# Scan stage of a hybrid SSD and ConvFFN layer: in-chunk products in pinned runs of four chunks, decay shift and clamp on ScalarE, state chain first in a step

## The chip, the cores and the metric

The kernel runs on one NeuronCore of a Trainium2 chip, as one launch. The metric is the device time of one execution in microseconds (us). A core has a matrix engine (TensorE, in the profile PE, with its weight loads as PEld), a vector engine (VectorE, DVE), a scalar engine (ScalarE, ACT), a general engine (GpSimd, POOL) and a queue processor that issues DMA transfers (SyncE, SP). Each takes its own instructions in order; semaphores tie them together. TensorE reads from the on-chip memory SBUF and writes to the banks of PSUM; the other compute engines move results out of PSUM.

## The reference

One layer of a flow-matching backbone with 1024 channels, for 1024 latent tokens and 128 context tokens. The part that matters here is the state space scan (SSD) of the first sub-layer. For each of 32 heads of 64 channels, each direction, and each chunk of 128 tokens:

```
a_cs = cumsum(dt * A) inside the chunk
L = exp(where(i >= j, a_cs[i] - a_cs[j], -inf))
CB = C @ B^T                                   (one per group of 8 heads)
y_diag = (CB * L) @ (x * dt)                   products inside the chunk
states = B^T @ (exp(a_cs[-1] - a_cs) * x * dt) what the chunk adds to the state
h[k+1] = exp(a_cs[-1]) * h[k] + states         the chain over chunks
y_off = (C * exp(a_cs)) @ h[k]                 what earlier chunks give
y = y_diag + y_off, both directions, + D * x
```

There are eight latent chunks, which start from a given state, and one context chunk, which starts from zero and whose final states are outputs. Before the scan stand a norm, a modulation and one input projection (`h @ w_in`), with a convolution and a SiLU on x, B and C. After it come a gate with SiLU(z), a gated norm, a second branch (a spatial gating MLP), the merge, and the ConvFFN.

## The kernel before, in words

**Number format.** Large products are made of three matmuls of split numbers (`gemm_cm`, L295 to L303: high times high, high times low, low times high). The products of the scan are plain float32 matmuls; the trace shows each of them as two records.

**Projection units.** One unit (`inproj`, L425) makes one tile of 128 output channels for all 1152 tokens, in three blocks of 384 tokens with 24 matmuls each (`gps`, 72 in all). There are three PSUM banks for them (`pg`). A unit's sink takes the block out of PSUM, and between blocks other work is emitted.

**The scan.** The 32 heads are handled as 16 pairs `q`. Pair q has tiles X (its x, channel-major, three buffers), Xtok (the same by tokens), and shares B, C and CB with its group of four pairs. The nine chunks are handled in five stages `s`: stages 0 to 3 have two latent chunks each, stage 4 is the context chunk. Parts of the work are:

- `ssd_loads` (L632): a DMA on SP's queue brings the cumulative sums into every partition (R, three buffers; E, two buffers), and the starting state into H.
- `mstage` (L662), the decays of one stage: R plus a bias per row (`nb`, which holds log dt minus the cumulative sum), limited to 60, through exp, times CB, both directions added into the first half of R. Of eight shifts of 128x128, the first NACT = 4 run on ScalarE and need a clamp of their own on VectorE (L677); the others do shift and clamp in one VectorE instruction (L674).
- `chain` (L697), in four steps: weighted x (`xwf`, `xwb`), its product with B into PSUM (`pst`, a single bank), then H[k+1] = decay * H[k] + product on VectorE.
- `ctx_state` (L717): the same for the context chunk (`pstc`, in the same single bank), out to the outputs.
- `main` (L729): the products with the state (`yo`, one bank), the products inside the chunks (`yd`, one bank; 64 columns wide, because each head has 64 channels, the two heads of a pair in the two column halves), then VectorE puts E * yo, D * x and yd together in X.

**Order of the work.** `pro` and `outs` (L765 to L767) list the steps of a pair; `merge` (L770) spreads the steps of outs(q) and pro(q+1) over the projection units of round q. The framework then orders each engine's instructions by priority, that is by place in the program, as soon as what they need is there in its own plan. `tc.high_priority(offset=P_SCAN)` moves the steps ahead of their place by 50; decays at the start have 200. `queue_behind` (L274) places one instruction behind another on its engine, without a semaphore. `z_unit(q-1)`, one round later, multiplies the finished X by SiLU(z) and stores it.

Of the kernel before, what the change touches and what calls it, by code (L numbers as in the profile page):

```python
# [14 lines left out]
NL = 1024  # L15
# [17 lines left out]

NGATE = [1, 1, 1, 0, 1, 1, 1, 0, 1, 1, 1, 0, 1, 1, 1, 0, 0]

NACT = 4

NXM, NWM, GBUF = 4, 10, 7

LAG0 = 12  # L40

LASTK = 4

P_SCAN, P_HT, P_MOD, P_DECAY = 50, 100, 200, 200


def gcol(t):
# [61 lines left out]
def body(tc, A, O):  # L109
# [338 lines left out]
    k_cm, kp = pool("tok")  # L448
    nb = kp.tile([128, NC, 64], F32, name="nb")
    wst = kp.tile([128, NC, 64], F32, name="wst")  # L450
    cdk = kp.tile([128, 8, 2, 32], F32, name="cdk")
    sb_cm, spb = pool("ssdB")
    u_cm, up = pool("dt")
# [29 lines left out]
    def decays():  # L483
        for src, dst in ((xd, dtt), (xa, adt)):
            ps = tbank("pdt")
            for i in range(4):
                PE.transpose(ps[:, 128 * i:128 * i + 128], src[:, 128 * i:128 * i + 128], ident)
            pv = ps.rearrange("p (c m) -> p c m", m=128)
            S.copy(dst[:, 0:4, :], pv[:, :, 0:64])
            V.tensor_copy(dst[:, 5:9, :], pv[:, :, 64:128])  # L490
        ps = tbank("pdt4")
        for j, src in enumerate((xd, xa)):
            PE.transpose(ps[:, 128 * j:128 * j + 128], src[:, 512:640], ident)
        for j, dst in enumerate((dtt, adt)):
            V.tensor_copy(dst[:, 4, :], ps[:, 128 * j:128 * j + 64])
        for d in range(2):
            a_d = adt[:, :, 32 * d:32 * d + 32]
            for lhs, dst in (((Lo, Up)[d], acst), (ones, tot)):
                pv = tbank(f"pacs{d}")[:, :288].rearrange("p (c h) -> p c h", h=32)
                PE.matmul(pv, lhsT=lhs, rhs=a_d, start=True, stop=True)  # L500
                V.tensor_copy(dst[:, :, 32 * d:32 * d + 32], pv)
        rows = up.tile([64, NC, 128], F32, name="rows")
        for b in range(3):
            ps = tbank(f"prow{b}")
            for i in range(3):
                PE.transpose(ps[:64, 128 * i:128 * i + 128], acst[:, 3 * b + i, :], ident)
            V.tensor_copy(rows[:, 3 * b:3 * b + 3, :], ps[:64, :384].rearrange("p (c m) -> p c m", m=128))
        for d in range(2):
            for h in range(2):
                SP.dma_start(acs_scr[:, d, h], rows[32 * d + h:32 * d + 32:2, :, :])  # L510
        V.tensor_scalar(lndt, dtt, 1e-18, None, op0=ALU.max)
        S.activation(lndt, lndt, AF.Ln)
        V.tensor_tensor(nb, lndt, acst, op=ALU.subtract)
# [115 lines left out]

    Rt, EPt, Ht = {}, {}, {}  # L630

    def ssd_loads(q, s):  # L632

        cc = cc_of(s)
        n = len(cc)
        R = spa.p.tile([128, 2, 2, 2, 128], F32, tag="R", name=f"R{q}{s}", bufs=3)
        if n == 2:
            SP.dma_start(R.rearrange("p d h c i -> p (d h) (c i)"),
                         acs_scr[q, :, :, cc[0]:cc[0] + 2].rearrange("d h c i -> (d h) (c i)").unsqueeze(0).to_broadcast([128, 4, 256]))
# [4 lines left out]
        if s < 4:  # L644
            E = spa.p.tile([128, 2, 2, 128], F32, tag="EP", name=f"EP{q}{s}", bufs=2)
            for h in range(2):
                SP.dma_start(E[64 * h:64 * h + 64].rearrange("p d c i -> p d (c i)"),
                             acs_scr[q, :, h, cc[0]:cc[0] + 2].rearrange("d c i -> d (c i)").unsqueeze(0).to_broadcast([64, 2, 256]))
            EPt[q, s] = E
        if s == 4:  # L650
            H = spa.p.tile([128, 8, 2, 128], F32, tag="H", name=f"H{q}", bufs=2)
            SP.dma_start(H[:, 0], A["h0"][q])
            Ht[q] = H

    def ssd(q):

# [1 line left out]
        _, Bt, CT, CB = groups[g]  # L658
        X, Xt = xq[q]
        Dc = par[:, P_D + q:P_D + q + 1]  # L660

        def mstage(s):  # L662
            cc = cc_of(s)
            n = len(cc)
            R = Rt[q, s]
            for d in range(2):
                for h in range(2):
                    col = 32 * d + 2 * q + h
                    for i, c in enumerate(cc):
                        r = R[:, d, h, i, :]  # L670
                        if 4 * d + 2 * h + i < NACT:
                            S.activation(r, r, AF.Identity, bias=nb[:, c, col:col + 1])  # L672
                        else:
                            V.tensor_scalar(r, r, nb[:, c, col:col + 1], 60.0, op0=ALU.add, op1=ALU.min)  # L674
            Rv = R.rearrange("p d h c i -> p (d h) c i")[:, :, :n]
            if NACT:
                V.tensor_scalar(Rv[:, :NACT // 2], Rv[:, :NACT // 2], 60.0, None, op0=ALU.min)  # L677
            S.activation(Rv, Rv, AF.Exp)
            if s < 4:
                S.activation(EPt[q, s], EPt[q, s], AF.Exp)  # L680
            for d in range(2):
                if n == 2:
                    r = R[:, d].rearrange("p h c i -> p h (c i)")
                    cb = CB[:, d, cc[0]:cc[0] + 2, :].rearrange("p c i -> p (c i)").unsqueeze(1).to_broadcast([128, 2, 256])
                else:
                    r = R[:, d, :, 0, :]
                    cb = CB[:, d, cc[0], :].unsqueeze(1).to_broadcast([128, 2, 128])
                V.tensor_tensor(r, r, cb, op=ALU.mult)
            V.tensor_tensor(R[:, 0, :, :n], R[:, 0, :, :n], R[:, 1, :, :n], op=ALU.add)

        def xw(c0, n, d, dst):

# [24 lines left out]
        def ctx_state():  # L717
# [7 lines left out]
            S.copy(so, ps[:, 0])  # L725
            for d in range(2):
                SP.dma_start(O[2 + d][0, 0, 2 * q:2 * q + 2].rearrange("h p n -> (h p) n"), so[:, d, :])

        def main(s):  # L729
            cc = cc_of(s)  # L730
            n = len(cc)
            R = Rt.pop((q, s))
            o = gcol(128 * cc[0])
            if s < 4:
                H = Ht[q]
                yo = pyo.tile([128, 2, 2, 128], F32, tag="yo", name=f"yo{q}{s}")
                for i, c in enumerate(cc):
                    for d in range(2):
                        k = c if d == 0 else 7 - c
                        PE.matmul(yo[:, d, i, :], lhsT=H[:, k, d, :], rhs=CT[:, 128 * c:128 * c + 128], start=True, stop=True)  # L740
            yd = pyd.tile([128, 512], F32, tag="yd", name=f"yd{q}{s}")[:, :128 * n]
            for i, c in enumerate(cc):
                for h in range(2):
                    PE.matmul(yd[64 * h:64 * h + 64, 128 * i:128 * i + 128], lhsT=Xt[:, c, 64 * h:64 * h + 64],  # L744
                              rhs=R[:, 0, h, i, :], start=True, stop=True, tile_position=(0, 64 * h))
            xv = X[:, o:o + 128 * n]
            if s < 4:
                E = EPt.pop((q, s))
                V.tensor_tensor(E, E, yo, op=ALU.mult)
                V.scalar_tensor_tensor(xv, xv, Dc, E[:, 0].rearrange("p c i -> p (c i)"), op0=ALU.mult, op1=ALU.add)  # L750
                V.tensor_tensor(xv, xv, E[:, 1].rearrange("p c i -> p (c i)"), op=ALU.add)
                V.tensor_tensor(xv, xv, yd, op=ALU.add)
            else:
                V.scalar_tensor_tensor(xv, xv, Dc, yd, op0=ALU.mult, op1=ALU.add)

        def nxt(s):
            if q + 1 < 16:
                ssd_loads(q + 1, s)

        def step(*fs):  # L760
            def run():
                for f, *a in fs:
                    f(*a)
            return run
        pro = [step((mstage, 4), (chain, 0)), step((mstage, 0), (chain, 1)), step((chain, 2)), step((chain, 3))]  # L765
        outs = [step((mstage, 1), (main, 4), (ssd_loads, q, 2)), step((mstage, 2), (main, 0), (ssd_loads, q, 3), (ctx_state,)),
                step((mstage, 3), (main, 1), (nxt, 4)), step((main, 2), (nxt, 0)), step((main, 3), (nxt, 1))]  # L767
        return pro, outs

    def merge(fills, steps):  # L770
# [35 lines left out]
    gtp.p, gtp.bufs = spa.p, 1  # L806
    run_unit(first_x)
    for s in (4, 0, 1):
        ssd_loads(0, s)
    after = None  # L810
    for q in range(17):
        steps = []
# [538 lines left out]
```

## Time and profile before

| What | us |
|---|---|
| median of three runs | 2472.48 (2471.34 to 2474.54) |
| the profiled execution | 2474.21 |
| its span, first to last instruction | 2472.1 |
| TensorE busy | 2428.6 |
| VectorE busy | 1853.4 |
| ScalarE busy | 1110.5 |

The span holds the instructions of the profiled execution; its own time is 2.1 us longer. A row of a group of instructions has the line, the engine, the operation, the tiles written and read, the shape and the count; after the bar the busy time in us, the mean of one in ns, then the engine's idle time before them and what ended it. A timeline row has the start, the time it covers, the engine, the line and operation, and the count of like instructions in a row. Matmuls overlap one another, so that a matmul's own duration is longer than the distance from its start to the next one's. A row of waits has the waiting engine and line, what it waited for, the total in us, the number of waits and the longest.

### The profile page before, as it was taken

Reading aid. Unit: us, or ns where it says so; the run is one execution under the profiler, and the core shown is the slowest. Engines: PE = TensorE matmul, PEld = TensorE weight load, DVE = VectorE, ACT = ScalarE, POOL = GpSimd, SP = SyncE. Lnnn points to the kernel's source line nnn. Section 1 sums busy time; section 2 is a strip of 40 time slices with the busy share of each in tenths; the row PEclk is TensorE's granted clock in tenths of the full one; section 3 lists DMA queues with packets and bytes.
Section 4 is the critical chain, followed back from the end, with each engine's and each line's share of the span. In section 5 each row is a group of like instructions: output and inputs, shape, how many; then the busy total and the mean of one; then the engine's idle time right before and its main releaser. Section 6 shows DMA issues by size and latency. Waiting matters only on the chain.

```text
span 2472.1 us, 37398 instructions
## 1 busy us (share of the span) xinstructions
PE 2428.6 (98%) x13951; PEld 2271.1 (92%) x13951; DVE 1853.4 (75%) x3150; ACT 1110.5 (45%) x2118; POOL 28.4 (1%) x82
## 2 busy tenths in 40 slices
PE   7989999999999999999999999999999999999998
PEld 5989999999999998899999998999999999998777
DVE  5668988878878884983546657459999989998554
ACT  5545655555555553211445545354333433344443
POOL 0000000000000000000000000000000000000000
PEclk9999999999999999999999999999999999999999
DMA  6134334433433444641456657442212221114674
GB/s 257 39 96 146 123 125 141 136 95 117 140 101 103 149 123 157 214 150 62 148 163 206 210 161 237 153 139 76 71 65 71 69 68 61 66 64 135 217 244 132
DMA packets 204182, 323.21 MB, mean 131 GB/s; under 512 B 19329, under 2 KB 113313, under 8 KB 203873
## 3 DMA queue, kind: packets, MB, share of 16 engines
q1 hardware_dynamic: 204000, 320.82, 40.5%
q8 instruction: 110, 1.80, 0.3%
q14 instruction: 72, 0.58, 0.1%
HBM read 278.22 MB, written 42.52 MB: 130 GB/s over the span
## 4 chain that ended last, share of the span: by engine, by line
PE 89%; DMA 6%; DVE 2%; ACT 1%; issue 1%; SPq 0%; POOL 0%; DVEq 0%; POOLq 0%; ACTq 0%
PE gps L301 10%; PE gps L303 10%; PE gps L302 10%; PE pup L302 7%; PE pup L303 7%; PE pup L301 7%; PE fo L1167 4%; PE fo L1169 4%; PE fo L1168 4%; PE yo L740 2%; PE yd L744 2%; PE pbs L301 2%; PE pbs L302 2%; PE pbs L303 2%; PE pv L865 1%; PE pv L866 1%
## 5 line engine op out<-in xcount | busy, mean ns | idle before, releaser
L85 DVE TENSOR_TENSOR wl<-wr,wh 128x512 fp32r<-128x512 f32 x544 | 371.7, 689 | 250.5 <-ACT wh L84 241.7
L84 ACT CAST wh<-wr 128x512 fp32r<-128x512 f32 x544 | 333.9, 619 | 471.3 <-PE pup L302 121.6
L301 PE MATMUL gps<-hh,wh 128*128 128x384 f32 x1512 | 518.2, 343 | 0.2 <-ACT pad L356 0.2
L303 PE MATMUL gps<-hh,wl 128*128 128x384 f32 x1512 | 513.9, 340 | 0.0
L302 PE MATMUL gps<-hl,wh 128*128 128x384 f32 x1512 | 513.4, 340 | 0.0
L1155 DVE SCALAR_TENSOR_TENSOR acc<-U,fpar,acc 128x960 f32<-128x960 f32 (+1 forms) x352 | 444.3, 1267 | 16.0 <-ACT acc L1148 8.2
L302 PE MATMUL pup<-h2l,wh 128*128 128x384 f32 x1056 | 353.1, 334 | 0.0
L301 PE MATMUL pup<-h2h,wh 128*128 128x384 f32 x1056 | 352.9, 334 | 0.0
L303 PE MATMUL pup<-h2h,wl 128*128 128x384 f32 x1056 | 352.4, 334 | 0.0
L301 PEld LDWEIGHTS gps<-hh,wh 128*128 128x128 f32 x1512 | 284.8, 188 | 6.4 <-issue 5.5
L302 PEld LDWEIGHTS gps<-hl,wh 128*128 128x128 f32 x1512 | 284.9, 188 | 3.9 <-issue 3.8
L303 PEld LDWEIGHTS gps<-hh,wl 128*128 128x128 f32 x1512 | 284.6, 188 | 4.1 <-issue 4.1
L301 PEld LDWEIGHTS pup<-h2h,wh 128*128 128x128 f32 x1056 | 198.2, 188 | 1.3
L302 PEld LDWEIGHTS pup<-h2l,wh 128*128 128x128 f32 x1056 | 198.2, 188 | 1.3
L303 PEld LDWEIGHTS pup<-h2h,wl 128*128 128x128 f32 x1056 | 198.2, 188 | 0.0
L1137 ACT COPY U<-pup 128x384 f32<-128x384 f32 (+1 forms) x132 | 58.4, 443 | 225.1 <-PE pup L303 225.1
L672 ACT ACTIVATE R<-R,nb 128x128 f32<-128x128 f32 x288 | 93.2, 391 | 136.6 <-DMA R<-acs_scr 132.5
L1167 PE MATMUL fo<-wh,gh 128*128 128x512 f32 x384 | 148.1, 397 | 0.3 <-ACT wh L84 0.3
L1168 PE MATMUL fo<-wh,gl 128*128 128x512 f32 x384 | 148.3, 396 | 0.0
L1169 PE MATMUL fo<-wl,gh 128*128 128x512 f32 x384 | 139.8, 396 | 0.0
L301 PE MATMUL pbs<-ysh,wh 128*128 128x384 f32 x384 | 129.8, 338 | 3.6 <-ACT wh L84 1.8
L303 PE MATMUL pbs<-ysh,wl 128*128 128x384 f32 x384 | 129.7, 338 | 0.2
(303 smaller groups left out, 3965.7 us busy)
## 6 DMA issues: line engine op xcount, KB each, us to landing
wr<-in_w_dn SPq DMA_DIRECT2D x132, 256.0 KB, 2.9
wr<-in_w_in SPq DMA_DIRECT2D x130, 256.0 KB, 2.9
R<-acs_scr SPq DMA_DIRECT2D x64, 512.0 KB, 4.1
wr<-in_w_bs SPq DMA_DIRECT2D x96, 256.0 KB, 3.4
wr<-in_w_up SPq DMA_DIRECT2D x90, 256.0 KB, 2.6
EP<-acs_scr SPq DMA_DIRECT2D x128, 128.0 KB, 3.2
wmt<-in_w_modt SPq DMA_DIRECT2D x32, 512.0 KB, 3.8
wr<-in_w_bu SPq DMA_DIRECT2D x48, 256.0 KB, 2.8
```

Source lines behind the costliest of these rows:

```text
L84: self.nc.scalar.copy(hi, w)
L85: self.nc.vector.tensor_tensor(lo, w, hi.bitcast(F32), op=ALU.subtract)
L301: PE.matmul(ps, lhsT=wh, rhs=xh, start=first and k == 0, stop=False)
L302: PE.matmul(ps, lhsT=wh, rhs=xl, start=False, stop=False)
L303: PE.matmul(ps, lhsT=wl, rhs=xh, start=False, stop=last and k == n - 1)
L672: S.activation(r, r, AF.Identity, bias=nb[:, c, col:col + 1])
L740: PE.matmul(yo[:, d, i, :], lhsT=H[:, k, d, :], rhs=CT[:, 128 * c:128 * c + 128], start=True, stop=True)
L1137: S.copy(u[:, a // 64:b // 64, 1:65], src.rearrange("p (r c) -> p r c", c=64))
L1155: tap = V.scalar_tensor_tensor(av[:, r0:r1], u[:, r0 + dy - 1:r1 + dy - 1, dx:dx + 64], w[i], av[:, r0:r1], op0=ALU.mult, op1=ALU.add)
L1167: PE.matmul(outs[c][h], lhsT=mh[:, cs_], rhs=wh, start=k == 0, stop=False)
L1168: PE.matmul(outs[c][h], lhsT=ml[:, cs_], rhs=wh, start=False, stop=False)
L1169: PE.matmul(outs[c][h], lhsT=mh[:, cs_], rhs=wl, start=False, stop=k == NFF - 1)
```

## The change

- **Runs.** The products inside the chunks leave `main` and become `within(b)`, for b = 0 and 1: four latent chunks at once into one full bank `yd`, and with b = 1 the context chunk too, whose result goes to the second half of the bank that holds `pstc`. All of a run's matmuls but the first are placed behind the first, at a priority offset of 400. One addition of 128x512 takes the place of two of 128x256.
- **RS.** The sum over both directions is written to a tile of its own (RS, for four chunks, two buffers) and not into R. R can be loaded anew after that addition.
- **Decays.** All shifts are ScalarE's: relu(nb - R) with nb = top + cumulative sum - log dt, then exp(top - that). This limits the exponent to `top`, the largest log dt, so that the limit of 60 and its VectorE instructions are gone. `top` is found once, by two reductions and a transpose.
- **Order.** `chain` stands ahead of `mstage` in a step. The loads of R, E and H are separate functions, placed apart; the exponential of E is made in `mstage` for stages 0 and 1, and in `main` for 2 and 3.

```
-NACT = 4
-P_SCAN, P_HT, P_MOD, P_DECAY = 50, 100, 200, 200
+P_SCAN, P_HT, P_MOD, P_DECAY, P_RUN = 50, 100, 200, 200, 400
...
-        V.tensor_tensor(nb, lndt, acst, op=ALU.subtract)
+        V.tensor_reduce(top, lndt.rearrange("p c m -> p (c m)"), axis=AX.X, op=ALU.max)
+        tops = up.tile([128, 128], F32, name="tops")
+        V.tensor_copy(tops, top.to_broadcast([128, 128]))
+        ps = tbank("ptop")
+        PE.transpose(ps[:, :128], tops, ident)
+        V.tensor_reduce(top, ps[:, :128], axis=AX.X, op=ALU.max)
+        V.tensor_tensor(nb, acst, lndt, op=ALU.subtract)
+        V.tensor_scalar(nb, nb, top, None, op0=ALU.add)
...
         def mstage(s):
-            R = Rt[q, s]
+            R = Rt.pop((q, s))
+            if s == 4:
+                RS[2] = spa.p.tile([128, 2, 1, 128], F32, tag="RSc", name=f"RSc{q}", bufs=2)
+            elif s % 2 == 0:
+                RS[s // 2] = spa.p.tile([128, 2, 4, 128], F32, tag="RS", name=f"RS{q}{s}", bufs=2)
+            sum_ = RS[s // 2][:, :, 2 * (s % 2):2 * (s % 2) + n]
...
-                        if 4 * d + 2 * h + i < NACT:
-                            S.activation(r, r, AF.Identity, bias=nb[:, c, col:col + 1])
-                        else:
-                            V.tensor_scalar(r, r, nb[:, c, col:col + 1], 60.0, op0=ALU.add, op1=ALU.min)
+                        S.activation(r, r, AF.Relu, scale=-1.0, bias=nb[:, c, col:col + 1])
-            if NACT:
-                V.tensor_scalar(Rv[:, :NACT // 2], Rv[:, :NACT // 2], 60.0, None, op0=ALU.min)
-            S.activation(Rv, Rv, AF.Exp)
+            S.activation(Rv, Rv, AF.Exp, scale=-1.0, bias=top)
...
-            V.tensor_tensor(R[:, 0, :, :n], R[:, 0, :, :n], R[:, 1, :, :n], op=ALU.add)
+            V.tensor_tensor(sum_, R[:, 0, :, :n], R[:, 1, :, :n], op=ALU.add)
...
         def ctx_state():
...
+            RS[3] = ps[:, 1, 0, :]
...
+        def main(s):
+            (yo products as before)
+            E = EPt.pop((q, s))
+            if s >= 2:
+                S.activation(E, E, AF.Exp)
+            V.tensor_tensor(E, E, yo, op=ALU.mult)
+            V.scalar_tensor_tensor(xv, xv, Dc, E[:, 0].rearrange("p c i -> p (c i)"), op0=ALU.mult, op1=ALU.add)
+            V.tensor_tensor(xv, xv, E[:, 1].rearrange("p c i -> p (c i)"), op=ALU.add)
+
+        def within(b):
+            yd = pyd.tile([128, 512], F32, tag="yd", name=f"yd{q}{b}")
+            todo = [(yd[:, 128 * i:128 * i + 128], 4 * b + i, RS[b][:, :, i]) for i in (2, 3, 0, 1)]
+            if b == 1:
+                yc = RS[3]
+                todo.append((yc, 8, RS[2][:, :, 0]))
+            first = None
+            with tc.high_priority(offset=P_RUN):
+                for p, c, r in todo:
+                    for h in range(2):
+                        m = PE.matmul(p[64 * h:64 * h + 64], lhsT=Xt[:, c, 64 * h:64 * h + 64], rhs=r[:, h, :],
+                                      start=True, stop=True, tile_position=(0, 64 * h))
+                        if first is None:
+                            first = m
+                        else:
+                            queue_behind(m, first)
+            xv = X[:, 512 * b:512 * b + 512]
+            V.tensor_tensor(xv, xv, yd, op=ALU.add)
+            if b == 1:
+                xv = X[:, gcol(NL):gcol(NL) + 128]
+                V.scalar_tensor_tensor(xv, xv, Dc, yc, op0=ALU.mult, op1=ALU.add)
...
-        pro = [step((mstage, 4), (chain, 0)), step((mstage, 0), (chain, 1)), step((chain, 2)), step((chain, 3))]
-        outs = [step((mstage, 1), (main, 4), (ssd_loads, q, 2)), step((mstage, 2), (main, 0), (ssd_loads, q, 3), (ctx_state,)),
-                step((mstage, 3), (main, 1), (nxt, 4)), step((main, 2), (nxt, 0)), step((main, 3), (nxt, 1))]
+        pro = [step((chain, 0), (mstage, 4)), step((chain, 1), (mstage, 0)), step((chain, 2)), step((chain, 3))]
+        outs = [step((mstage, 1), (load_R, q, 2)), step((mstage, 2), (main, 0), (load_R, q, 3), (load_E, q, 2), (ctx_state,)),
+                step((mstage, 3), (main, 1), (within, 0), (load_E, q, 3), (nxt, load_R, 4), (nxt, load_H)),
+                step((main, 2), (nxt, load_R, 0), (nxt, load_E, 0)), step((main, 3), (within, 1), (nxt, load_R, 1), (nxt, load_E, 1))]
```

More of the change, by code (lines that the diff above doesn't have):

```diff
@@ L450, in body @@
     wst = kp.tile([128, NC, 64], F32, name="wst")
+    top = kp.tile([128, 1], F32, name="top")
     cdk = kp.tile([128, 8, 2, 32], F32, name="cdk")
@@ L630, in body, with load_R @@
     Rt, EPt, Ht = {}, {}, {}
-    def ssd_loads(q, s):
+    def load_R(q, s):
         cc = cc_of(s)
-        n = len(cc)
         R = spa.p.tile([128, 2, 2, 2, 128], F32, tag="R", name=f"R{q}{s}", bufs=3)
-        if n == 2:
+        if len(cc) == 2:
             SP.dma_start(R.rearrange("p d h c i -> p (d h) (c i)"),
@@ L643, in ssd_loads, with load_E, load_H @@
         Rt[q, s] = R
[L644 to L653, printed above, removed]
+    def load_E(q, s):
+        cc = cc_of(s)
+        E = spa.p.tile([128, 2, 2, 128], F32, tag="EP", name=f"EP{q}{s}", bufs=2)
+        for h in range(2):
+            SP.dma_start(E[64 * h:64 * h + 64].rearrange("p d c i -> p d (c i)"),
+                         acs_scr[q, :, h, cc[0]:cc[0] + 2].rearrange("d c i -> d (c i)").unsqueeze(0).to_broadcast([64, 2, 256]))
+        EPt[q, s] = E
+    def load_H(q):
+        H = spa.p.tile([128, 8, 2, 128], F32, tag="H", name=f"H{q}", bufs=2)
+        SP.dma_start(H[:, 0], A["h0"][q])
+        Ht[q] = H
     def ssd(q):
@@ L660, in ssd @@
         Dc = par[:, P_D + q:P_D + q + 1]
+        RS = {}
         def mstage(s):
@@ L670, in mstage @@
                         r = R[:, d, h, i, :]
-                        if 4 * d + 2 * h + i < NACT:
-                            S.activation(r, r, AF.Identity, bias=nb[:, c, col:col + 1])
-                        else:
-                            V.tensor_scalar(r, r, nb[:, c, col:col + 1], 60.0, op0=ALU.add, op1=ALU.min)
+                        S.activation(r, r, AF.Relu, scale=-1.0, bias=nb[:, c, col:col + 1])
             Rv = R.rearrange("p d h c i -> p (d h) c i")[:, :, :n]
-            if NACT:
-                V.tensor_scalar(Rv[:, :NACT // 2], Rv[:, :NACT // 2], 60.0, None, op0=ALU.min)
-            S.activation(Rv, Rv, AF.Exp)
+            S.activation(Rv, Rv, AF.Exp, scale=-1.0, bias=top)
             if s < 4:
-                S.activation(EPt[q, s], EPt[q, s], AF.Exp)
+                exp_E(s)
             for d in range(2):
@@ L688, in mstage, with exp_E @@
                 V.tensor_tensor(r, r, cb, op=ALU.mult)
-            V.tensor_tensor(R[:, 0, :, :n], R[:, 0, :, :n], R[:, 1, :, :n], op=ALU.add)
+            V.tensor_tensor(sum_, R[:, 0, :, :n], R[:, 1, :, :n], op=ALU.add)
+        def exp_E(s):
+            if s < 2:
+                S.activation(EPt[q, s], EPt[q, s], AF.Exp)
         def xw(c0, n, d, dst):
@@ L727, in ctx_state @@
                 SP.dma_start(O[2 + d][0, 0, 2 * q:2 * q + 2].rearrange("h p n -> (h p) n"), so[:, d, :])
+            RS[3] = ps[:, 1, 0, :]
         def main(s):
             cc = cc_of(s)
[L731 to L740, printed above, removed]
@@ L741, in main @@
-            yd = pyd.tile([128, 512], F32, tag="yd", name=f"yd{q}{s}")[:, :128 * n]
-            for i, c in enumerate(cc):
[L743 to L754, printed above, removed]
@@ L756, in nxt @@
-        def nxt(s):
+            o = 128 * cc[0]
+            H = Ht[q]
+            yo = pyo.tile([128, 2, 2, 128], F32, tag="yo", name=f"yo{q}{s}")
+            for i, c in enumerate(cc):
+                for d in range(2):
+                    k = c if d == 0 else 7 - c
+                    PE.matmul(yo[:, d, i, :], lhsT=H[:, k, d, :], rhs=CT[:, 128 * c:128 * c + 128], start=True, stop=True)
+            xv = X[:, o:o + 256]
+            E = EPt.pop((q, s))
+            if s >= 2:
+                S.activation(E, E, AF.Exp)
@@ new lines, in main @@
+            V.tensor_tensor(E, E, yo, op=ALU.mult)
[10 more added lines that the diff above has]
+                for p, c, r in todo:
+                    for h in range(2):
+                        m = PE.matmul(p[64 * h:64 * h + 64], lhsT=Xt[:, c, 64 * h:64 * h + 64], rhs=r[:, h, :],
[9 more added lines that the diff above has]
+                V.scalar_tensor_tensor(xv, xv, Dc, yc, op0=ALU.mult, op1=ALU.add)
@@ L757, in nxt @@
+        def nxt(f, *a):
             if q + 1 < 16:
-                ssd_loads(q + 1, s)
+                f(q + 1, *a)
         def step(*fs):
@@ L808, in body @@
     for s in (4, 0, 1):
-        ssd_loads(0, s)
+        load_R(0, s)
+        if s < 4:
+            load_E(0, s)
+    load_H(0)
     after = None
```

## The prediction

> **What bounds the kernel now.** I read the page first, then the engines by stage, then the scan (the head products, 150 to 950 us) matmul by matmul.
>
> ```profile
> span 2472.1 us, 37398 instructions
> ...
> PE 89%; DMA 6%; DVE 2%; ACT 1%; issue 1%; SPq 0%; POOL 0%; DVEq 0%; POOLq 0%; ACTq 0%
> ...
> 450.00:550.00 100.00, 100.00 (x618) 93.14 (x617) 79.34 (x166) 52.05 (x102) 0.49 (x5) 1.00 0.37 111
> ```
>
> The columns of the last row are window, its length, then PE, PEld, DVE, ACT, POOL, clock, DMA share, GB/s. TensorE is on the end's chain, is busy all through the scan, and its clock is full. VectorE has 21 us of room in these 100, ScalarE 48. But a busy TensorE can still be a slow one, so I set its instruction counts against its own pace. The scan from 160 to 945 us:
>
> ```profile
> L301 PE MATMUL gps<-hh,wh 128*128 128x384 f32 x1106 | 378.8, 342 | 0.0
> L303 PE MATMUL gps<-hh,wl 128*128 128x384 f32 x1107 | 377.6, 341 | 0.0
> L302 PE MATMUL gps<-hl,wh 128*128 128x384 f32 x1106 | 376.6, 340 | 0.0
> L740 PE MATMUL yo<-CT,H 128*128 128x128 f32 x503 | 72.3, 277 | 0.0
> L744 PE MATMUL yd<-R,Xtok 128*64 128x128 f32 x556 | 58.1, 288 | 0.0
> L709 PE MATMUL pst<-xwf,Btok 128*128 128x128 f32 x218 | 43.1, 279 | 0.0
> L710 PE MATMUL pst<-xwb,Btok 128*128 128x128 f32 x218 | 42.6, 277 | 0.0
> L549 PE MATMUL ptX<-cst,X 128*128 128x128 f32 x126 | 18.9, 274 | 0.8 <-ACT Xtok L550 0.8
> L724 PE MATMUL pstc<-Btok,xwc 128*128 128x128 f32 x64 | 9.9, 275 | 0.0
> L571 PE MATMUL pcb<-CT,BT 128*128 128x128 f32 x54 | 7.2, 275 | 0.0
> L549 PE MATMUL ptB<-cst,BT 128*128 128x128 f32 x27 | 4.3, 278 | 0.0
> ```
>
> The mean durations overlap; the pace is read from starts. Timeline rows (start, time, engine, operation), in three places:
>
> ```profile
> 518.23 0.34 PE L303 MATMUL gps<-hh,wl 128*128 128x384 f32 x1
> ...
> 524.64 0.34 PE L301 MATMUL gps<-hh,wh 128*128 128x384 f32 x1
> ```
> ```profile
> 838.97 0.34 PE L302 MATMUL gps<-hl,wh 128*128 128x384 f32 x1
> 839.24 0.66 PE L744 MATMUL yd<-R,Xtok 128*64 128x128 f32 x8
> 839.83 0.44 PE L303 MATMUL gps<-hh,wl 128*128 128x384 f32 x1
> 840.11 0.34 PE L301 MATMUL gps<-hh,wh 128*128 128x384 f32 x1
> ...
> 840.63 1.05 PE L740 MATMUL yo<-CT,H 128*128 128x128 f32 x8
> 841.54 0.55 PE L549 MATMUL ptX<-cst,X 128*128 128x128 f32 x3
> ```
> ```profile
> 504.58 0.45 PE L301 MATMUL gps<-hh,wh 128*128 128x384 f32 x1
> 504.96 0.43 PE L744 MATMUL yd<-R,Xtok 128*64 128x128 f32 x2
> ...
> 506.79 0.44 PE L301 MATMUL gps<-hh,wh 128*128 128x384 f32 x1
> ```
>
> The first pair spans 37 starts: 6.41 / 37 = 0.1732 us per gps. Eight yo records take 0.91 us to the start of what follows, 0.113 each; a float32 product is two such records, and I give that pace to every full-width float32 record. yd is quicker, since its two heads use different column halves and overlap: a stretch of eight records lasts 0.66 us (839.24), one of four 0.44 (150.68, below), so a further record costs 0.22 / 4 = 0.055. Now the sum over the window: 3319 gps x 0.1732 = 574.9; 503 + 218 + 218 + 64 + 54 + 126 + 27 = 1210 float32 records x 0.113 = 136.7; 556 yd x 0.055 = 30.6. Together 742.2 of 785 us. **42.8 us are TensorE time that no instruction accounts for.**
>
> Where they are: around yd, whose 64-column form (128*64) is the only one of its kind here. From the gps at 838.97 to that at 840.11 are 1.14 us; two gps and eight yd explain 0.346 + 0.44, so entering and leaving the form cost 0.36 us. Where single products alternate with gps, from 504.58 to 506.79, each of three rounds of one gps and one product (two yd records) takes 2.21 / 3 = 0.737 us, less 0.173 and 0.11: 0.454 us. Listed through the scan there are 109 such stretches, from
>
> ```profile
> 150.68 0.44 PE L744 MATMUL yd<-R,Xtok 128*64 128x128 f32 x4
> ...
> 947.89 0.66 PE L744 MATMUL yd<-R,Xtok 128*64 128x128 f32 x8
> ```
>
> the first to the last. 109 x 0.36 to 0.454 is 39 to 49 us: the whole 42.8, with nothing left for other waits.
>
> **The change part by part.**
>
> *Pinned runs (within).* 16 pairs of heads q, two runs each: 8 products, then 10 with the context chunk. The products stay the same; stretches fall from 109 to 32, which keep 32 x 0.36 = 11.5 us. Removed: 42.8 + 1 (the stretches outside the window) - 11.5 = **32 us**, on the path that sets the end. All inputs are there when the run's first product can go (chunks 2 and 3, the latest, stand first, and the rest is ordered behind it), and the offset of 400 puts the run ahead of any projection matmul in flight, so I take the runs as unbroken; two stretches for each run would take back 11.5 us.
>
> *What a run waits for.* One run needs four chunks of RS instead of two of R, and the single yd bank given back by the preceding addition. R makes no run late as I read it: a buffer of R is now free after the RS addition on VectorE instead of after yd, RS has two buffers, so the decays run ahead. The bank is the tight one already:
>
> ```profile
> 842.24 0.42 DVE L752 TENSOR_TENSOR X<-X,yd 128x256 f32<-128x256 f32 x1
> ...
> 843.11 0.66 PE L744 MATMUL yd<-R,Xtok 128*64 128x128 f32 x8
> ```
>
> Given back at 842.66, taken at 843.11: 0.45 us to spare, without a wait on TensorE (idle 0.0 in the yd row above). One switch of 0.36 us in that loop goes away, so about 0.1 us remains and some runs will wait. I take 0.1 us x 32 = 3 us; ends 0 and, if each run is as late as ScalarE is for its R loads (1.9 us, below), 61 us.
>
> *Shift and clamp on ScalarE.*
>
> ```profile
> L672 ACT ACTIVATE R<-R,nb 128x128 f32<-128x128 f32 x288 | 93.2, 391 | 136.6 <-DMA R<-acs_scr 132.5 <-PE gps L303 2.3 <-PE yd L744 1.7
> ...
> 812.61 1.28 ACT L672 ACTIVATE R<-R,nb 128x128 f32<-128x128 f32 x4 [3.89 <-DMA R<-acs_scr]
> ...
> 522.08 0.88 DVE L674 TENSOR_SCALAR R<-R,nb 128x128 f32<-128x128 f32 x4 [0.82 <-DMA R<-acs_scr]
> ...
> L677 DVE TENSOR_SCALAR R<-R 128x512 f32<-128x512 f32 (+1 forms) x80 | 31.5, 394 | 3.8 <-ACT R L672 3.4
> ...
> ACT R L672 <- DMA R<-acs_scr: 132.5, 69, 5.3
> ```
>
> VectorE's 288 shifts move at 1.28 / 4 = 0.32 us: +92 us on ScalarE over the scan's 800 us, from 52 to 63.5 in 100. VectorE loses 288 x 0.22 = 63 and the clamps' 31.5, from 79 to 67.5. Neither is on the path: cost 0, covered by TensorE's 48 us for each q (worked out below). No Relu stands in this trace; its nearest row is the Identity of the same shape. Between 0.22 (VectorE's) and 0.39 (the row's mean) ScalarE ends between 60 and 66 in 100, far under TensorE either way.
>
> [...]
>
> A Relu outside the loaded function table would cost table loads: the row is
>
> ```profile
> L512 ACT ACT_TABLE_LOAD x1 | 1.3, 1283 | 0.0
> ```
>
> so 1.28 us, two for each of 80 decay steps: 205 us, ScalarE at 90 in 100. No load stands between Identity, Exp and Tanh in the scan, so I take 0. [...]
>
> *The maximum (top).* Two reductions, a copy, a transpose and one more pass on nb come before the first shift.
>
> ```profile
> 124.60 0.75 DVE L513 TENSOR_TENSOR nb<-lndt,acst 128x576 f32<-128x576 f32 x1
> ...
> 135.17 0.69 ACT L672 ACTIVATE R<-R,nb 128x128 f32<-128x128 f32 x2 [5.07 <-DMA R<-acs_scr]
> ```
>
> At 0.75 us or less each they are about 3 us, and nb, ready at 125.35, has 9.8 us until its first reader, which waits for a DMA. I take 1 us, should they get ahead of work that the DMA waits for; ends 0 and 4. If that cover were gone, they cost their 3 us once.
>
> *The order of steps and loads.* chain comes before mstage, the loads of R, E and H are separate, E's Exp moves into main for s of 2 and 3. The chain's matmuls wait 0.0 us on TensorE now (the pst rows), so there is nothing to gain; the exponentials that move keep their 128x512 form and count. On SP's queue, R loads now wait for yd:
>
> ```profile
> SPq L638 <- PE yd L744: 101.9, 37, 6.6
> ```
>
> that becomes a wait for an earlier addition, and an E load that waits no longer stands ahead of the next R. Behind it on that queue stand weight loads, so they too leave sooner; no credit is taken, since TensorE waits for neither. H's load goes to the end of its step, behind one R load; its first reader is the next step: 0.
>
> *The state bank.* The context product goes into the bank of pstc, so chain(q+1) can start only when that is read after within(q, 1).
>
> ```profile
> 797.44 0.38 PE L709 MATMUL pst<-xwf,Btok 128*128 128x128 f32 x2
> ...
> 858.69 0.41 DVE L752 TENSOR_TENSOR X<-X,yd 128x256 f32<-128x256 f32 x1
> ```
>
> From the first chain product to the release that within(q, 1) needs (842.66) are 45.2 us, while TensorE's round for one q (three projection tiles of 72 records, and a sixteenth of the counts of yo, pst, pstc, ptX and yd, two switches) is 216 x 0.1732 + 73 x 0.113 + 36 x 0.055 + 0.7 = 48.3 us. It fits, barely: 0.
>
> Sum: -32 + 3 + 1 = -28 us. The profiled execution is 2474.21 us (span 2472.1 and 2.1 around it), so 2446; the runs' median, 2472.48, lies 1.7 us lower: **2444.5 us** is forecast, from 2434 (the price of a switch at 0.454 before, no waits) to 2457 by its own bounds.
>
> **The rivals.** *Runs break* because another matmul of equal rank slips in: 64 stretches, 11.5 us back, 2456. For it: today's single products alternate with gps. Against: 400 is far from 50.
>
> *Runs wait, slower.* A pinned run stands at the head of TensorE's queue, and all projection matmuls stand behind it. ScalarE waits 132.5 us for R in 69 waits, 1.9 us each; were every run that late, 32 x 1.9 = 61 us: 2444.5 - 3 + 61 = 2502.5. The place is the first record of each run, the price its idle time, and it decides from 31 / 32 = 1.0 us a run. For it: decays are now all on ScalarE, in order, behind those waits. Against: decays run ahead by two buffers, and today's tight bank costs no wait. At about that 1.0 us it gives *no change*, 2472.
>
> *The state bank serialises.* If the context product is read only behind main(3), the loop is 797.44 to 859.10 = 61.7 us against 48.3; 12 rounds of three units lose 13.4 each, less one round of lead: +113, 2557.5. Against: that read needs only the run.
>
> **How the numbers follow.** Forecast 0.58, and 0.05 for better than 2434; broken runs 0.10; no change 0.08; waiting runs 0.14; the state bank 0.05. A measurement of this kernel tells 0.2%, 5 us, from no change. Faster: 0.58 + 0.05 + 0.10 = 0.73; same 0.08; slower 0.19. The range runs from 2434 to 2474, over the broken runs and into no change; outside are 0.19 above and a little below.
>
> **What would show it.** Right: 32 yd stretches of 16 and 20 records; the same sum over the scan leaves some 11 to 15 us; its end moves about 30 us forward; no Relu table load; ScalarE near 65 and VectorE near 70 in 100. Wrong: idle time of TensorE before yd above 1 us a run, or before pst.

## The result, and the profile after

The changed kernel takes 2451.48 us (median of four runs, 2449.09 to 2454.71), the kernel before 2473.51 beside it on the same chip: a ratio of 0.991, 95% interval 0.9893 to 0.9928. That is 22 us faster; forecast were 2444.5 us and 28. The profiled execution took 2452.29 us.

The page's span and chain, and two windows (columns as in the prediction), of the kernel after:

```profile
span 2450.2 us, 37307 instructions
...
PE 88%; DMA 6%; DVE 3%; ACT 2%; issue 1%; SPq 0%; POOL 0%; DVEq 0%; ACTq 0%; POOLq 0%
...
150.00:900.00 750.00, 747.52 (x5043) 732.73 (x5042) 575.20 (x1056) 503.83 (x1103) 3.45 (x35) 1.00 0.41 127
450.00:550.00 100.00, 100.00 (x677) 98.21 (x676) 74.83 (x136) 60.01 (x126) 0.49 (x5) 1.00 0.39 115
```

The same long window of the kernel before:

```profile
150.00:900.00 750.00, 749.20 (x4869) 709.11 (x4868) 620.27 (x1388) 410.89 (x799) 3.77 (x34) 1.00 0.40 122
```

TensorE is still what the end waits for. Over the scan ScalarE goes from 55 to 67 busy in 100, VectorE from 83 to 77.

Now the sum of the prediction over the changed scan, from 160 us to the first product behind it (`pv`, 935.05 us). Groups of instructions of the kernel after in that window:

```profile
L301 PE MATMUL gps<-hh,wl 128*128 128x384 f32 x1126 | 383.4, 341 | 0.0
L299 PE MATMUL gps<-hh,wh 128*128 128x384 f32 x1125 | 382.1, 340 | 0.0
L300 PE MATMUL gps<-hl,wh 128*128 128x384 f32 x1125 | 381.9, 339 | 0.0
L755 PE MATMUL yo<-CT,H 128*128 128x128 f32 x510 | 71.1, 275 | 0.0
L725 PE MATMUL pst<-xwf,Btok 128*128 128x128 f32 x218 | 42.3, 275 | 1.1 <-DVE H L731 1.0
L726 PE MATMUL pst<-xwb,Btok 128*128 128x128 f32 x218 | 42.1, 275 | 0.0
L775 PE MATMUL yd<-RS,Xtok 128*64 128x128 f32 x496 | 33.9, 279 | 0.0
L556 PE MATMUL ptX<-cst,X 128*128 128x128 f32 x126 | 19.5, 273 | 1.4 <-DVE X L535 1.4
L740 PE MATMUL pstc<-Btok,xwc 128*128 128x128 f32 x64 | 9.9, 275 | 0.0
L578 PE MATMUL pcb<-CT,BT 128*128 128x128 f32 x54 | 7.3, 277 | 0.0
L775 PE MATMUL pstc<-RSc,Xtok 128*64 128x128 f32 x64 | 6.2, 273 | 0.0
L556 PE MATMUL ptB<-cst,BT 128*128 128x128 f32 x27 | 4.6, 274 | 0.0
```

At the paces of before: 3376 x 0.1732 = 584.7; 1217 x 0.113 = 137.5; 560 of 64 columns x 0.055 = 30.8. Together 753.0 of 775.05 us, so 22 are left. Where they are, the end of the scan tells. Timeline rows of TensorE, kernel after (in brackets the idle time before, and what ended it):

```profile
924.05 0.34 PE L301 MATMUL gps<-hh,wl 128*128 128x384 f32 x1
924.32 1.09 PE L775 MATMUL yd<-RS,Xtok 128*64 128x128 f32 x16
925.24 0.39 PE L775 MATMUL pstc<-RSc,Xtok 128*64 128x128 f32 x4
925.56 0.44 PE L299 MATMUL gps<-hh,wh 128*128 128x384 f32 x1
925.84 0.34 PE L300 MATMUL gps<-hl,wh 128*128 128x384 f32 x1
926.01 0.33 PE L301 MATMUL gps<-hh,wl 128*128 128x384 f32 x1
926.19 1.05 PE L755 MATMUL yo<-CT,H 128*128 128x128 f32 x8
935.05 0.80 PE L900 MATMUL pv<-vwh,hh 128*128 128x512 f32 x1 [7.82 <-ACT vwh L82]
935.64 0.63 PE L901 MATMUL pv<-vwh,hl 128*128 128x512 f32 x1
...
939.91 0.63 PE L901 MATMUL pv<-vwh,hl 128*128 128x512 f32 x1
...
940.94 0.40 PE L901 MATMUL pv<-vwh,hl 128*128 128x512 f32 x1
...
941.86 0.40 PE L902 MATMUL pv<-vwl,hh 128*128 128x512 f32 x1
```

The run is unbroken: 16 records and the context chunk's 4. From 924.05 to 925.84 are 1.79 us; two `gps` and 20 records explain 0.346 + 1.10, so the switch (into the 64-column form and back) costs 0.34. There are 32 such stretches. The other large part is new: the last projection stands at 926.01, the last `yo` runs out at 927.1 (eight records at 0.113), and TensorE then waits until 935.05, 8.0 us. Without it 14 us are left, about the 31 stretches in the window (11.2). `pv` then starts at half pace: ten starts in 4.27 us (0.43 each) against four in 0.92 (0.23) from 940.94; the 13 starts before 940.70 lose 2.6 us. The granted clock of that stretch is half, too:

```profile
935.00:940.70 5.70, 5.65 (x13) 4.51 (x14) 1.90 (x3) 1.04 (x2) 0.00 (x0) 0.51 1.03 329
```

What the wait is for, VectorE and ScalarE of the kernel after:

```profile
927.33 0.69 DVE L760 TENSOR_TENSOR EP<-EP,yo 128x512 f32<-128x512 f32 x1 [0.98 <-PE yo L755]
...
929.03 0.69 DVE L782 TENSOR_TENSOR X<-X,yd 128x512 f32<-128x512 f32 x1
929.76 1.22 DVE L604 TENSOR_TENSOR X<-X,z 128x1024 f32<-128x1024 f32 x1
```
```profile
931.01 1.06 ACT L605 ACTIVATE z<-X 128x1024 f32<-128x1024 f32 x1 [4.32 <-DVE X L604]
932.10 1.26 ACT L607 ACTIVATE X<-X,par 128x1153 f32<-128x1153 f32 x1
933.26 1.22 ACT L617 COPY gt<-gps 128x384 f32<-128x384 f32 x3
934.36 1.68 ACT L82 CAST vwh<-wr 128x512 fp32r<-128x512 f32 x3
```

It is the drain of the last pair: its additions, its gate and its scaling, the copies of the last projection's blocks (`gt`), and behind them in ScalarE's order the cast of the weights for `pv`. The kernel before has the same order:

```profile
944.99 1.05 PE L740 MATMUL yo<-CT,H 128*128 128x128 f32 x8
```
```profile
953.30 1.15 ACT L84 CAST vwh<-wr 128x512 fp32r<-128x512 f32 x2
```

The cast stands 8.3 us behind the start of the last `yo` there and 8.2 after. Before, this time was covered: the last run started at 947.89 and projections went on to 955.9. So the projections end 30 us sooner (926.0 against 955.9), the pairs only 20 (their last addition starts at 929.0 against 948.6), and the first `pv` 20.9 (935.1 against 956.0).

### The profile page after: what moved, and what is told of

Its sections match the earlier page's. It is cut to its first block, busy times and chain, and to the rows that moved or that the text cites. A ratio compares the mean times of both kernels' runs of the same rounds, so it can differ in the third digit from the quotient of the medians.

```text
span 2450.2 us, 37307 instructions
## 1 busy us (share of the span) xinstructions
PE 2398.8 (98%) x13952; PEld 2268.6 (93%) x13952; DVE 1783.1 (73%) x2754; ACT 1190.7 (49%) x2406; POOL 28.0 (1%) x82
## 3 DMA queue, kind: packets, MB, share of 16 engines
q8 instruction: 109, 1.79, 0.3%
## 4 chain that ended last, share of the span: by engine, by line
PE 88%; DMA 6%; DVE 3%; ACT 2%; issue 1%; SPq 0%; POOL 0%; DVEq 0%; ACTq 0%; POOLq 0%
PE gps L299 11%; PE gps L301 11%; PE gps L300 11%; PE pup L300 7%; PE pup L301 7%; PE pup L299 7%; PE fo L1202 3%; PE fo L1203 3%; PE fo L1204 3%; PE yo L755 2%; PE pbs L301 2%; PE pbs L299 2%; PE pbs L300 2%; PE pv L900 1%; PE yd L775 1%; PE pv L901 1%
## 5 line engine op out<-in xcount | busy, mean ns | idle before, releaser
L688 ACT ACTIVATE R<-R,nb 128x128 f32<-128x128 f32 x576 | 178.0, 392 | 39.0 <-DMA R<-acs_scr 36.6
```

Of the source, the lines that this page charges most:

```text
L688: S.activation(r, r, AF.Relu, scale=-1.0, bias=nb[:, c, col:col + 1])
```

## The experiments

Each edits the changed kernel. Ratios are to the kernel before on the same chip, with 95% intervals. "Left over" is the time from 160 us to the first `pv` that TensorE's paces don't explain, counted gap by gap, and split into what stands at the 64-column stretches (to the second start behind each) and all other gaps: before 42.6 + 3.0, after 10.9 + 13.3. Counted with the paces of the sum above, the totals are 2 us lower throughout (43.6 before, 22.2 after); the differences are the same.

**No pinned runs.**

```
-P_SCAN, P_HT, P_MOD, P_DECAY, P_RUN = 50, 100, 200, 200, 400
+P_SCAN, P_HT, P_MOD, P_DECAY, P_RUN = 50, 100, 200, 200, 0
...
-                        if first is None:
-                            first = m
-                        else:
-                            queue_behind(m, first)
```

> The changed kernel without the pinning: the products of within stay in one function, but at the steps' own offset of 50 and without being placed behind the first. Switch theory: they alternate with projection matmuls again, between 60 and 150 stretches, each 0.36 to 0.454 us: 12 to 40 us longer than the changed kernel unless the lag at the end shrinks by its 10 us: 2455 to 2485 us. If the stretches are not what costs: 2449 to 2453 us whatever their number.

Measured: 2481.78 us, 1.002 (1.001 to 1.0029). The stretches are 133 again, left over 57.3 + 1.4. TensorE in this run:

```profile
926.69 0.43 PE L775 MATMUL yd<-RS,Xtok 128*64 128x128 f32 x2
927.06 0.45 PE L300 MATMUL gps<-hl,wh 128*128 128x384 f32 x1
927.43 0.43 PE L775 MATMUL yd<-RS,Xtok 128*64 128x128 f32 x2
```

Single products alternate with projections again, 0.74 us a round. (57.3 - 10.9) / 101 stretches = 0.46 us each, the upper of the two prices of the prediction. The expected 12 to 40 us for the stretches hold. All other parts of the change together gain nothing: without the pins and their offset the kernel is 0.2% slower than before.

**Decays as before**: four of eight shifts and the clamps back on VectorE, limit 60, no `top`.

```
...
-                        S.activation(r, r, AF.Relu, scale=-1.0, bias=nb[:, c, col:col + 1])
+                        if 4 * d + 2 * h + i < 4:
+                            S.activation(r, r, AF.Identity, bias=nb[:, c, col:col + 1])
+                        else:
+                            V.tensor_scalar(r, r, nb[:, c, col:col + 1], 60.0, op0=ALU.add, op1=ALU.min)
...
-            S.activation(Rv, Rv, AF.Exp, scale=-1.0, bias=top)
+            V.tensor_scalar(Rv[:, :2], Rv[:, :2], 60.0, None, op0=ALU.min)
+            S.activation(Rv, Rv, AF.Exp)
```

> The changed kernel with the decays' shift and clamp as they were (four shifts on ScalarE with a clamp on VectorE, four on VectorE, limit 60, no top). If the move to ScalarE is hidden, as predicted: 2449 to 2454 us. If VectorE's lighter load is what lets the runs go without waits: waits before yd and a later scan end, 2455 to 2475 us. If ScalarE's longer list makes the scan late: 2440 to 2447 us.

Measured: 2521.59 us, 1.0184 (1.0168 to 1.0201): some 70 us slower than the changed kernel, slower than before, and outside all three of the expected ranges. Left over 25.4 + 69.6. Its waits of TensorE (total, number, longest), then two windows:

```profile
PE pst L721 <- DVE H L727: 34.8, 5, 9.8
```
```profile
150.00:900.00 750.00, 714.64 (x4713) 700.49 (x4713) 599.32 (x1300) 403.90 (x784) 3.38 (x34) 0.97 0.38 119
250.00:350.00 100.00, 82.79 (x544) 80.29 (x543) 75.10 (x153) 49.12 (x91) 0.40 (x4) 0.88 0.33 99
```

VectorE is no fuller than in the kernel before (80 in 100), yet TensorE waits for the chain. One pair's chain on VectorE in this experiment, and its first and last addition in the kernel after:

```profile
488.17 0.41 DVE L727 TENSOR_TENSOR H<-H,pst 128x256 f32<-128x256 f32 x1
...
492.10 0.87 DVE L683 TENSOR_SCALAR R<-R,nb 128x128 f32<-128x128 f32 x4
...
517.90 0.41 DVE L727 TENSOR_TENSOR H<-H,pst 128x256 f32<-128x256 f32 x1
```
```profile
478.75 0.41 DVE L731 TENSOR_TENSOR H<-H,pst 128x256 f32<-128x256 f32 x1
...
498.12 0.41 DVE L731 TENSOR_TENSOR H<-H,pst 128x256 f32<-128x256 f32 x1
```

Between the additions stand shifts (L683), clamps and sums of the decays. A pair's seven additions span 29.7 us here and 19.4 in the kernel after; over the pairs but the first, the means are 28.1 and 22.8. The kernel before has 28.0 as well, so the chain is not slower than it was; what is new must lie in what stands beside it. The next experiment shows the shared bank to be a part of that. From the second pair's first chain product to the last pair's, a pair takes 53.8 us here (210.7 to 963.4, 14 passes) and 49.4 in the kernel after (197.7 to 889.1). The window's clock of 0.88 adds half pace behind the waits: after 5.9 us of waiting, at 507.8, the chain's pairs of `pst` records start 0.43 us apart, where they start 0.22 apart at 498.1.

**The same with a bank of its own for the context product** (the edit of the next experiment beside it).

> The decays as they were (half of the shifts and the clamps on VectorE) together with the context product in a bank of the pool of two. The decays as they were took 2521.6 us, with a loop of 54 us a pair for TensorE's 48. Bank theory (the hold on the bank of pstc makes the pairs a chain, and VectorE's work inside it sets its length): without the hold two pairs overlap again, and the time falls to 2445 to 2470 us, whatever VectorE has to do. VectorE theory (the decays' instructions among the chain's, all waiting for the same buffers, are too many by themselves): it stays at 2500 us or more.

Measured: 2488.9 us, 1.0052 (1.0039 to 1.0065), between the two theories. TensorE still waits for the chain, 19.2 us in five waits, the longest 8.6.

33 of the 70 us go with the shared bank, and 38 remain against the changed kernel with a bank apart (2450.64, below). Neither theory alone holds: the shared bank, which costs about 1 us in the changed kernel (below), costs 33 where the chain is slow, and the decays on VectorE cost 38 without it. The chain's additions span 29.9 us here. By what the 38 come about is not shown: the kernel before ran a chain of 28.0 us without such waits, and its order of steps and loads was not tried beside the old decays.

**The context product in a bank of its own.**

```
-            RS[3] = ps[:, 1, 0, :]
...
-                yc = RS[3]
+                yc = tbank(f"yc{q}")[:, :128]
```

> The changed kernel, but the context product of within(1) goes into a bank of the pool of two (tbank) and not into the bank of pstc, so that chain of the next pair need not wait for it. Bank theory: the first chain product of a pair starts 5 to 15 us before the previous pair's read of the context product (now 3 us after it), the last pair is done before the projection units are, TensorE's wait of 7.8 us before the first pv row falls under 1 us and the half clock after it (2.6 us) goes too: about 2441 us. E theory (the last pair's main steps are held by the two E buffers): the wait stays at 6 us or more, 2449 to 2453 us. Either way 32 stretches of yd.

Measured: 2450.64 us, 0.9892 (0.9876 to 0.9908); left over 15.5 + 8.3, with 35 stretches and not 32, since three of the runs leave their context products apart. Against the changed kernel this is 1 us by the medians and 4 by the ratios, and the intervals overlap. The shared bank orders the pairs, in the kernel after:

```profile
838.02 0.34 DVE L785 SCALAR_TENSOR_TENSOR X<-X,par,pstc 128x128 f32<-128x128 f32 x1
```
```profile
841.49 0.38 PE L725 MATMUL pst<-xwf,Btok 128*128 128x128 f32 x2
```

The next pair's chain starts 3.1 us after the context product is read; in the kernel before it had started (842.28) while two additions of the old pair were still to come, the last at 858.69. With a bank of its own the chain starts 8 to 9 us ahead of that read (827.0 against 835.8), and the wait before `pv` falls from 8.0 to 1.4 us, both as the theory of the bank has it. But the wait does not fall because `pv` comes sooner. In this experiment:

```profile
925.12 1.05 PE L754 MATMUL yo<-CT,H 128*128 128x128 f32 x8
...
934.00 0.50 PE L899 MATMUL pv<-vwh,hh 128*128 128x512 f32 x1 [1.23 <-ACT vwh L82]
```

The last `yo` and the first `pv` stand 1.1 us sooner than in the kernel after, and 8.9 us apart in both; what moved is the projections, of which the last now stands at 932.4. A pair takes as long as with the shared bank, 49.3 us against 49.4 (second to last pair). And new waits stand earlier:

```profile
PE yd L774 <- DVE X L781: 3.6, 2, 1.9
```
```profile
841.59 0.42 DVE L729 TENSOR_TENSOR H<-H,cdk 128x256 f32<-128x256 f32 x1 [2.98 <-DMA H<-in_h]
841.93 0.68 DVE L781 TENSOR_TENSOR X<-X,yd 128x512 f32<-128x512 f32 x1
```

The next pair's chain now begins while the addition that frees the `yd` bank is still queued behind it on VectorE, and the chain waits for its load of H. The run waits for both.

**The loads of H earlier.** The next pair's load is issued at the start of the pair's first output step, the first pair's before its other loads.

```
-        outs = [step((mstage, 1), (load_R, q, 2)), ...
+        outs = [step((nxt, load_H), (mstage, 1), (load_R, q, 2)), ...
...
-                step((mstage, 3), (main, 1), (within, 0), (load_E, q, 3), (nxt, load_R, 4), (nxt, load_H)),
+                step((mstage, 3), (main, 1), (within, 0), (load_E, q, 3), (nxt, load_R, 4)),
```

> The changed kernel with the load of the next pair's starting state (H) first in the first of the outs steps, and first of the loads at the start; nothing else. Load theory (H now lands after VectorE has come to it, and what stands behind that instruction is late): VectorE's 19.0 us of waits for H fall under 2 us, TensorE's waits of 3.7 us before the first yo and 1.2 us before a pst go, the pairs follow faster and the wait of 8.0 us before pv shrinks: 2442 to 2447 us. If the bank of pstc alone holds the pairs apart: H waits go, the wait before pv stays at 7 us or more, 2447 to 2451 us.

Measured: 2447.88 us, 0.9896 (0.9877 to 0.9914), left over 11.9 + 11.8. VectorE's waits for H are 23.7 us in 14 waits here, 19.0 in 11 in the kernel after, and the wait before `pv` is the same 8.0 us.

TensorE's 3.7 us at the first `yo` are gone, but 2.6 for Xtok and 1.2 before a `pst` stand in the same place; and VectorE's waits for H are not gone, so that neither theory holds as it was put. An earlier place in the program did not bring H sooner where VectorE needs it. What holds those transfers is open; the buffer of H that they go to was not varied.

**Both** (bank and H).

> Both edits: the context product in a bank of the pool of two, and H loaded early. Theory that the two together make the time lost beside the switches (13.3 us of TensorE's time that no instruction and no switch explains, from 160 us to pv): it falls to 2 to 5 us, TensorE's yd waits for the bank (3.6 us with the first edit alone) go as well: 2440 to 2444 us. Rival (something else in the scan, such as the E buffers or the decays on ScalarE, sets its end): the unexplained time stays at 8 us or more, 2447 to 2452 us.

Measured: 2447.76 us, 0.9893 (0.9876 to 0.9909), left over 14.2 + 7.4. The time lies in the rival's range, the 7.4 us of other gaps between the numbers of the two, and 2.3 us of `yd`'s waits for the bank are still there: the theory that bank and H together make the lost time falls, and what else does is not told.

**Three buffers for E.**

```
-tag="EP", name=f"EP{q}{s}", bufs=2)
+tag="EP", name=f"EP{q}{s}", bufs=3)
```

> The changed kernel with three E buffers for two, nothing else. Bank theory: the main steps get closer (3 us apart for 5), which shortens each pair's loop by some 5 us and so also the lag at the end: the wait before pv falls by a part, 2445 to 2451 us. E theory: the wait before pv goes away wholly: 2441 us. If neither sets the lag: 2451 us.

Measured: 2453.52 us, 0.99 (0.9885 to 0.9915); the wait before `pv` is the same 8.0 us. The theory that late loads of E hold the last pair falls, and so does the part that the bank theory gave to this buffer.

**One unit of the gate moved from round 14 to round 16**, to put projections beside the drain.

```
-NGATE = [1, 1, 1, 0, 1, 1, 1, 0, 1, 1, 1, 0, 1, 1, 1, 0, 0]
+NGATE = [1, 1, 1, 0, 1, 1, 1, 0, 1, 1, 1, 0, 1, 1, 0, 0, 1]
```

> The changed kernel with one gate projection unit moved from round 14 to round 16 (the order of the units alone, the same work), so that 12.5 us of projection matmuls stand beside the last pair's scan. If the time lost is a scan that ends after its cover, whatever makes it late: the wait before pv falls under 1 us, clock full, about 2441 us. If the wait has to do with the weights of v themselves: it stays near 8 us, 2451 us. Rounds without the gate may show a small wait in the scan, 1 to 3 us.

Measured: 2451.73 us, 0.9893 (0.9878 to 0.9907), and the wait again 8.0: the last projection now stands at 922.0, the first `pv` at 933.4. A later place did not carry projections into the drain, so the first expectation failed. The second, of a wait that has to do with the weights of v, came as it was put: the cast of these weights stands behind the drain here too (932.7 us, 8.3 behind the start of the last `yo`). No run moves that cast ahead of the drain, so what it is worth is open.

**The old order in a step**, decays ahead of the chain.

```
-        pro = [step((chain, 0), (mstage, 4)), step((chain, 1), (mstage, 0)), ...
+        pro = [step((mstage, 4), (chain, 0)), step((mstage, 0), (chain, 1)), ...
```

> The changed kernel with the decays ahead of the state chain in the first two steps, as before. Predicted as worth nothing: 2449 to 2454 us. If the chain is what sets the pace of the pairs, as the chain of waits of the changed kernel shows at the end, a later chain lengthens each loop: the wait before pv grows to 12 us or more, 2455 to 2465 us.

Measured: 2445.02 us, 0.9877 (0.9862 to 0.9891), left over 10.9 + 10.5; the wait before `pv` is 6.1 us. Its interval ends just under that of the changed kernel, and it is faster than either expectation had it.

**The old order with H early.**

> The changed kernel with H loaded early and the decays ahead of the chain, the bank of pstc as it is. If the two are separate: 2441 us; if both act on VectorE's waits for H (a chain that comes later meets a state that has landed): 2444 to 2447 us, as with the decays ahead alone, and VectorE's waits for H are small in both.

Measured: 2450.98 us, 0.9896 (0.9882 to 0.9909), left over 11.9 + 11.0, slower than both expectations. The gain of the old order alone isn't there, so that single gain is not firm; and VectorE's waits for H are 19.3 us with the old order and 21.1 here, not small.

**All three: own bank, H early, the old order.**

> The changed kernel with three edits: context product in a bank of the pool of two, H loaded early, decays ahead of the chain. If their gains are separate (0.8, 3.6 and 6.5 us): 2441 us. If they all shorten the same wait at the end: 2444 to 2448 us.

Measured: 2443.44 us, 0.9867 (0.9853 to 0.988), left over 12.5 + 5.9. The time lies between the numbers of the two theories; the idle time before the first `pv` is 1.1 us.

It is the fastest kernel here, 33 us below the kernel before, and its interval lies under that of the changed kernel (0.9893 to 0.9928). The first `pv` stands at 927.4, and the last `yo` starts at 917.1 where it starts at 926.2 in the kernel after.

**The same with three buffers for E.**

> The three edits and three E buffers. If the E loads are what remains of the loop once the bank is free: the main steps come 3 us apart for 5, the wait before pv goes, 2438 to 2442 us. If not: as without the third buffer, or 2 us longer, as the third buffer alone was.

Measured: 2446.03 us, 0.9879 (0.9864 to 0.9894), left over 16.0 + 8.2. A third buffer helps no more than it did alone.

## Why the prediction was right, and where not

**Pinned runs, -32 us.** Right in mechanism and size. Stretches fall from 109 to 32, their left-over from 42.6 to 10.9 us, and taking the pins and their offset alone away gives more than the whole gain back (27 us by the ratios, 30 by the medians). What failed is the half sentence behind it, below. The rows here have 0.34 us for a stretch between projections and 0.46 for one among alternating ones; what TensorE does in that time they do not show.

**Runs wait 0.1 us each, +3 us.** Too high: the `yd` row after has idle 0.0. The rival of waiting runs is refuted for this kernel, though the wait that it names does come up in the experiment with the bank apart (3.6 us).

**Shift and clamp, "neither is on the path: cost 0".** No cost shows, as forecast: ScalarE has 67 busy in 100, and its shifts wait less for R than before:

```profile
L688 ACT ACTIVATE R<-R,nb 128x128 f32<-128x128 f32 x576 | 178.0, 392 | 39.0 <-DMA R<-acs_scr 36.6 <-DVE xwf L710 1.4 <-DVE X L762 0.6
...
L524 ACT ACT_TABLE_LOAD x1 | 1.3, 1283 | 0.0
```

No table load stands between the one of line 524 (120.5 us) and the next, of line 987 (965.4 us), behind the scan. VectorE was forecast near 70 in 100 and is at 77: it loses 45 us in 750, where the prediction took 94.5 from 800, and started from the 79 of the window from 450 to 550 us alone; what makes the difference was not broken down. But "neither is on the path" was read from the kernel before, and it fails beside the other parts: with the decays left on VectorE the changed kernel is 70 us slower. VectorE's busy share (80 in 100 against 83 before) does not show that. The decays' instructions stand among the chain's, which takes 28 us a pair and not 23; but the kernel before has 28 as well, so this place alone does not explain it. Shown are the two parts, 33 us with the shared bank and 38 without. One shift is quicker on VectorE (0.22 us against 0.32 on ScalarE, by the rows of the prediction); still, in this kernel the half of them that stays there makes it slower by these 70 us.

**"On the path that sets the end": 32 us counted in full.** This is the step that failed. The 32 us did come off TensorE's work in the scan, and the projections end 30 us sooner. But the end hangs on the first `pv`, and that on the cast of its weights, behind the last pair's drain on ScalarE; the last pair comes only 20 us sooner. Its drain had been covered by 7 us of projections; these now end before it, and 8.0 us of wait come in, which the sum put at nothing. The first `pv` stands 8.9 us behind the start of the last `yo` in the kernel after, with the bank apart and with the old order, whether TensorE waits there for 8.0, 1.4 or 6.1 us. Why the last pair gains only 20 us stays open: no edit of bank, H, E or order alone brings its last `yo` more than 2.4 us sooner in the profiles, the three of bank, H and order together 9.1.

**The state bank, "it fits, barely: 0".** It fits as forecast. The hold, put at 45.2 us, is 41.9 (796.4 to 838.4), and the passes from 796.4 to 841.5 and on to 889.1 take 45.1 and 47.6 us; TensorE waits there for no `pst`. With a bank of its own the time falls by 1 us, not clear of noise. The price holds only beside a quick chain: with the old decays the same bank costs 33 us.

**Chain first and the loads, "nothing to gain".** No gain shows. The old order was faster by itself and not with H early, so whether the new one costs a few us stays open. H's load was put at 0. TensorE waits 3.7 us for it at the first `yo` (142.2 us), but the kernel before waits 4.9 in the same place (141.8 us) for Xtok, so no cost shows; VectorE waits 19 us for it, and what of that reaches the end is not shown.

**The maximum, +1 us.** The first shift starts at 136.27 us against 135.17: 1.1. What of it reaches the end is not shown; in both kernels that shift waits for a DMA.

So the sum: -31.7 at the stretches, +8.0 before `pv`, +2.3 in the other gaps of the scan give -21.4; measured at the first `pv` are -20.9. From there to the end of the span are 1515.1 us against 1516.1, so it ends 21.9 us sooner. Of the signs named beforehand, the 32 stretches came and no table load did; the sum leaves 22 us and not 11 to 15, and the scan ends 21 us sooner and not 30. The 2.6 us of half pace do not show in that: ten us behind the first `pv`, a product (`prs`) waits for a load, 3.2 us before and 1.3 after. With the bank apart `pv` starts at full pace (its first product takes 0.50 us, 0.80 in the kernel after), and `prs` waits 3.9 us; it stands 10.3 us behind the first `pv` there and in the kernel after.

## What to carry to other kernels

When TensorE is busy all the time, set its counts against its own pace: here 43 us lay in the switches between two forms of matmul, and ordering the small products in unbroken runs brought 32 of them. Before counting a gain in full, ask which serial chain ends behind the engine that gets faster, what covered its end until now, and where the next stage's first instruction stands in the order of the other engines. And price a move to another engine with the other edits in place: a bank held one step longer cost 1 us beside a quick chain and 33 beside a slow one.

## What was not expected of the hardware

After 8.0 us without a matmul, TensorE ran at half pace for the next 5.65 us (0.43 us a start against 0.23), at a granted clock of 0.51. The clock was 1.00 from 927.2 to 930.3 us, 0.50 from 930.4 to 940.6, so already inside the wait, and 1.00 from 940.7 on. Half pace stood too behind the 5.9 us of the decays as before (0.43 us for a pair of `pst` records against 0.22), and in the kernel before behind 4.9 us at 141.8 (projections 0.32 us apart up to 147.56, then 0.17); behind the 1.4 us of the bank apart `pv` started at full pace. What sets the clock, and how long a wait it takes, is not shown. The wait of 8.0 us thus cost TensorE 2.6 us more than its length, a third; the time of the kernel did not feel that third, since the same stage waits for a load (1.3 us ahead of `prs`, 3.2 in the kernel before).
